# The order of the weight sums on VectorE in a feed-forward product by Strassen-like block sums

## The chip, the cores and the metric

The kernel runs on one core of one Trainium2 chip. Its matrix engine is TensorE (PE in the profile, with its weight loads as PEld); VectorE (DVE) and ScalarE (ACT) do the elementwise work, GpSimd (POOL) hardly any, and SyncE (SP) issues the DMAs. Each engine works through its own queue in order, and waits for the others by semaphores. The metric is the device time of one execution in microseconds.

## The reference

One layer of an encoder on 512 tokens of width 2048: a modulated norm, a mixer of two head groups, an output projection with a gated residual, and then the part this case is about, a SwiGLU feed-forward with D_FF = 5632:

```python
h = rms_norm(x, norm2_g[layer]) * (1.0 + sc2) + sh2
gate, up = jnp.split(h @ w_ffn_in[layer], 2, axis=-1)
x = x + g2 * ((jax.nn.silu(gate) * up) @ w_ffn_out[layer])
```

`h @ w_ffn_in` is the first feed-forward product, the multiplication by `w_ffn_out` the second. All is float32.

## The kernel before

**Float32 from three passes.** TensorE runs on a rounded float32 format. Every weight block is split into a high part, which is a cast on ScalarE (line 231), and a remainder, the block minus its high part, a subtraction on VectorE (line 232). The activations are split the same way beforehand. `product` (line 917) then multiplies high by high, high by remainder and remainder by high: for one product of 8 slices 24 matmuls of 128x128 by 128x256, all issued at line 93.

**Seven products in place of eight.** The columns of the hidden layer are worked off in 44 tiles of 128 gate columns and 128 up columns. The weights of a tile are four blocks of half the input width, A11 and A12 (gate, tile `wg`) and A21 and A22 (up, tile `wu`), and the tokens are in two halves of 256. Strassen's scheme in Winograd's form makes the 2x2 block product from seven half-size products and some sums. The sums of the activations are made once, before the loop. The sums of the weights are made for each tile on VectorE, in place: S1 = A21 + A22 (line 1138, in a buffer `ffS` of its own, one of three), A21 = A11 - A21 (1139), A11 = S1 - A11 (1140), A12 = A12 - A11 (1141).

**The loop over tiles** runs f from 2 to 43 (tiles 0 and 1 are done beforehand). In tile f the products come in the order 1, 2, 6, 7, 5, 4, 3, so that number 4 is the sixth in order. Product 1 uses A11 as loaded, 2 uses A12 as loaded, 6 the new A11, 7 the new A21, 5 S1, 4 A22, 3 the new A12. They go into three accumulators: A takes 1, 6, 5, 3; B takes 2; C takes 7 and 4. Where the scheme needs what an accumulator holds at some point, ScalarE copies it out (`tap`, line 1030): a after product 1, b after 6, c after 7, u after 5. The next product into the same accumulator may not start before the copy is done, so product 5 waits for the copy of b, product 4 for that of c.

**The tail of a tile** joins the taps: sg = B + a on VectorE (1163) and SiLU of it on ScalarE (1164), up = u + c (1165) and C + b (1166), SiLU of A (1167). `keep` (line 1078) multiplies the two (1084 for even tiles, 1086 for odd ones), makes four sums of each pair of tiles (1092 to 1096), splits them (1105 on ScalarE, 1106 on VectorE) and stores them through SP to memory (1108) as the operands of the second product. These jobs are spread over the next tiles by `one_later`. As B and a are complete early in the loop body's own tile, line 1163 of tile f runs in tile f itself; the final parts run in the next.

**Modulation rows.** While rows are left (tiles 2 to 17), the loop body ends with one row of the modulation, a load of 1 MB and a multiply with a sum of 2048 columns on VectorE (line 179, `ada`).

**Buffers for raw loads.** `wg`, `wu` and `ada` loads (1 MB each) share four buffers in turn. A buffer is free when its last reader is done: that of `wu` after the remainder of product 4, that of `wg` after the remainder of product 3, that of `ada` after line 179.

**What sets the order.** The kernel is traced as a program, and a scheduler orders each engine's queue: among the instructions whose inputs it takes to be ready it issues the one with the highest priority. Priority is the place in the program, and `high_priority(offset=n)` moves a block n places ahead. A tile is about 200 instructions, so with AHEAD = 300 the weight sums and the splits of a tile may be issued more than a tile early; taps stand at twice that. Line 1163 has no such offset. The scheduler works from its own estimates of when loads land. Once issued, a queue keeps that order on the chip. `issue_after(ins)` adds an edge of order alone: what the block traces on the engine of `ins` is queued behind `ins`.

```python
A21, A22 = halves_of(load(a["w_fi"][f, 1], [P, KT, P], f"wu{f}"))
S1 = tp.tile([P, HALF, P], F32, tag="sum", name=f"ffS{f}", bufs=3)
...
with tc.high_priority(offset=AHEAD):
    V.tensor_add(S1, A21, A22)
    V.tensor_sub(A21, A11, A21)
    V.tensor_sub(A11, S1, A11)
    V.tensor_sub(A12, A12, A11)
```

`split` (line 224) leaves in `last_lo` the subtraction that made the latest remainder.

Of the kernel before, what the change touches and what calls it, by code (L numbers as in the profile page):

```python
# [129 lines left out]
def trunk(ctx, tc, a):  # L130
    nc = tc.nc
    V, S, G = nc.vector, nc.scalar, nc.gpsimd
# [11 lines left out]
    def acc(name):  # L144
        return psum.tile([P, T], F32, tag="acc", name=name)

    def att(name):
        return psum.tile([P, T], F32, tag="att", name=name, bufs=2)
# [55 lines left out]
    def load(src, shape, name):  # L204
        r = raw_tile(shape, name + "r")
        nc.sync.dma_start(r, src)
        return r

    spare, count, home, last_lo = [], [0], [0], [None]
# [14 lines left out]
    def split(r, shape, name):  # L224
        count[0] += 1
        if spare and count[0] % 4 == 0:
            hi, lo = spare[0](shape, name)
        else:
            hi, lo = ring_pair(shape, name)
        with tc.high_priority(offset=AHEAD):  # L230
            S.copy(hi, r)  # L231
            last_lo[0] = V.tensor_sub(lo, r, hi.bitcast(F32)).ins  # L232
        return hi, lo
# [683 lines left out]
    def product(out, w, p, first=False):  # L917
        whi, wlo = w
        for j in range(HALF):
            PE.matmul(out, whi[:, j], H[p][:, j, 0], start=first and j == 0, stop=False, skip_group_check=True)  # L920
            PE.matmul(out, whi[:, j], H[p][:, j, 1], start=False, stop=False, skip_group_check=True)
            PE.matmul(out, wlo[:, j], H[p][:, j, 0], start=False, stop=j == HALF - 1, skip_group_check=True)
# [95 lines left out]
    def halves_of(r):  # L1018
        return r[:, 0:HALF], r[:, HALF:KT]

    def operand(raw, name, aside=True):
        home[0] = 48 if aside else 0
        return split(raw, [P, HALF, P], name)
# [3 lines left out]
    def tap(src, name):  # L1027
        t = tp.tile([P, HT], F32, tag="tap", name=name, bufs=4)
        with tc.high_priority(offset=2 * AHEAD):
            last_tap[0] = S.copy(t, src).ins  # L1030
        return t
# [24 lines left out]
    def begin_second():  # L1056
        places.append(fh.tile([P, 4, 4, 2, HT], F32R, tag="b1", name="opsA"))
        load_op(0, 0)
        load_y(0, 2)
        load_op(0, 1)  # L1060
        load_y(0, 0)
        yraw.append(hp.tile([P, 3, 4, T], F32, tag="hhi", name="yraw0"))
        load_y(0, 1)
        load_y(0, 3)
        load_op(0, 2)
        load_op(0, 3)
        places.append(hp.tile([P, 4, 4, 2, HT], F32R, tag="hlo", name="opsB"))
        for q in range(4, 7):
            load_op(0, q)
        yraw.append(fg.tile([P, 2, 4, T], F32, tag="b22", name="yraw"))  # L1070
# [7 lines left out]
    def keep(f, sg, up):  # L1078
        sgv, upv = (t.rearrange("p (h t) -> p h t", h=2) for t in (sg, up))
        if f % 2 == 0:  # L1080
            forms[0] = rp.tile([P, 8, HT], F32, tag="forms", name=f"forms{f}", bufs=1)
        R = forms[0]
        if f % 2 == 0:
            V.tensor_mul(R[:, 0:8:7], sgv, upv)
            return
        V.tensor_mul(R[:, 1:4:2], sgv, upv)
        n = f // 2
        c = max(c for c in range(len(CHUNKS)) if starts[c] <= n)

        def sums(a):  # L1090
            if a == 0:
                V.tensor_add(R[:, 4], R[:, 7], R[:, 3])
                V.tensor_sub(R[:, 5], R[:, 4], R[:, 0])
            else:
                V.tensor_sub(R[:, 6], R[:, 0], R[:, 7])
                V.tensor_sub(R[:, 2], R[:, 1], R[:, 5])

        def parts(a, b):
            q = slice(a, b)
            if f < FM - 1:  # L1100
                hi = tp.tile([P, b - a, HT], F32R, tag=f"fhi{a % 5}", name=f"fhi{f}_{a}", bufs=1)
            else:
                hi = cond[:, a * HT:b * HT].rearrange("p (q t) -> p q t", q=b - a).bitcast(F32R)
            with tc.issue_after(last_tap[0]):
                S.copy(hi, R[:, q])
            V.tensor_sub(R[:, q].bitcast(F32R), R[:, q], hi.bitcast(F32))  # L1106
            for i, t in enumerate((hi.bitcast(F32), R[:, q])):
                nc.sync.dma_start(opd[c][:, q, n - starts[c], i * HT:i * HT + HT], t)

        later.extend([partial(sums, 0), partial(sums, 1), partial(parts, 0, 3), None, partial(parts, 3, 5), None, partial(parts, 5, 7)])  # L1110
# [3 lines left out]
    def one_later():  # L1114
        job = later.pop(0) if later else None
        if job is not None:
            job()
# [10 lines left out]
    for f in range(2):  # L1128
        keep(f, held[:, 2 * f], held[:, 2 * f + 1])

    for f in range(2, FM):
        A11, A12 = halves_of(load(a["w_fi"][f, 0], [P, KT, P], f"wg{f}"))
        A21, A22 = halves_of(load(a["w_fi"][f, 1], [P, KT, P], f"wu{f}"))
        S1 = tp.tile([P, HALF, P], F32, tag="sum", name=f"ffS{f}", bufs=3)
        A, B, C = acc(f"ffA{f}")[:, 0:HT], acc(f"ffB{f}")[:, 0:HT], att(f"ffC{f}")[:, 0:HT]
        w1, w2 = operand(A11, f"ff{f}_1"), operand(A12, f"ff{f}_2")
        with tc.high_priority(offset=AHEAD):
            V.tensor_add(S1, A21, A22)
            V.tensor_sub(A21, A11, A21)
            V.tensor_sub(A11, S1, A11)  # L1140
            V.tensor_sub(A12, A12, A11)
        product(A, w1, 1, True)
        ta = tap(A, f"a{f}")
        one_later()
        product(B, w2, 2, True)
        one_later()
        product(A, operand(A11, f"ff{f}_6"), 6)
        tb = tap(A, f"b{f}")
        one_later()
        product(C, operand(A21, f"ff{f}_7"), 7, True)  # L1150
        t_c = tap(C, f"c{f}")
        one_later()
        product(A, operand(S1, f"ff{f}_5"), 5)
        tu = tap(A, f"u{f}")
        one_later()
        product(C, operand(A22, f"ff{f}_4"), 4)
        one_later()
        product(A, operand(A12, f"ff{f}_3", False), 3)

        sg = tp.tile([P, T], F32, tag="sg", name=f"sg{f}", bufs=2)  # L1160
        up = tp.tile([P, T], F32, tag="up", name=f"up{f}", bufs=1)
        with tc.high_priority(offset=2 * AHEAD if f == FM - 1 else 0):
            V.tensor_add(sg[:, 0:HT], B, ta)
            S.activation(sg[:, 0:HT], sg[:, 0:HT], AF.Silu)
            V.tensor_add(up[:, HT:T], tu, t_c)
            V.tensor_add(up[:, 0:HT], C, tb)
            S.activation(sg[:, HT:T], A, AF.Silu)
        if f == FM - 1:
            begin_second()
        with tc.high_priority(offset=2 * AHEAD if f == FM - 1 else 0):  # L1170
            keep(f, sg, up)
        if rest:
            rest.pop(0)()
# [20 lines left out]
    C = [wide[:, 0:T], wide[:, T:2 * T]]  # L1194
# [183 lines left out]
```

## Time and profile before

| | us |
|---|---|
| median of 3 runs | 2268.96 (2266.91 to 2269.43) |
| the profiled execution | 2268.31 |
| its span, first to last instruction | 2266.5 |
| tiles 7 to 43 of the first feed-forward product | 1103.70 to 1827.44 in the span |

The profile is one execution, recorded by instruction. Engines are busy or idle; where an engine sat idle before an instruction, the row says in brackets for how long and what released it. In rows of the timeline the first number is the start from the span's start and the second the duration. Neighbouring instructions of one engine overlap a little, so the step from start to start is shorter than the duration. `ff_5lo` and `ff_5hi` are the remainder and the cast of product 5; where the program's names have been shortened, `ff<-wu7r,ff` on line 232 is a remainder made from tile 7's `wu` (its first is product 7's, its second product 4's), and `ff<-wg7r,ff` one from `wg` (products 1, 2, 6 and 3 in this order). On PE the products are told by accumulator and operand: `ffA<-opA` is 1, `ffB<-opA` 2, `ffA<-opB` 6, `ffC<-opB` 7, `ffA<-opC` 5, `ffC<-opC` 4, `ffA<-opD` 3.

### The profile page before, as it was taken

Reading aid. Unit: us, or ns where it says so; the run is one execution under the profiler, and the core shown is the slowest. Engines: PE = TensorE matmul, PEld = TensorE weight load, DVE = VectorE, ACT = ScalarE, POOL = GpSimd, SP = SyncE. Lnnn points to the kernel's source line nnn. Section 1 sums busy time; section 2 is a strip of 40 time slices with the busy share of each in tenths; the row PEclk is TensorE's granted clock in tenths of the full one; section 3 lists DMA queues with packets and bytes.
Section 4 is the critical chain, followed back from the end, with each engine's and each line's share of the span. In section 5 each row is a group of like instructions: output and inputs, shape, how many; then the busy total and the mean of one; then the engine's idle time right before and its main releaser. Section 6 shows DMA issues by size and latency. Waiting matters only on the chain. (4 is left out here: it accounts for less than half of the span.)

```text
span 2266.5 us, 35532 instructions
## 1 busy us (share of the span) xinstructions
PE 2221.9 (98%) x14171; PEld 2025.4 (89%) x14171; DVE 1912.1 (84%) x2566; ACT 1157.3 (51%) x2015; POOL 10.1 (0%) x25
## 2 busy tenths in 40 slices
PE   7999899999999999999999999999999999999999
PEld 6899899978888888899999999999999987788887
DVE  8886778899888875599899988888888888898888
ACT  4315666566565622475444545555455554545453
POOL 0000000000000000000000000000000000000000
PEclk9999999999999999999999999999999999999999
DMA  9885546763232296326565554535454486666452
GB/s 371 314 319 215 178 142 232 288 228 112 93 112 75 83 327 250 111 103 228 205 215 201 195 181 145 176 131 177 142 172 150 159 333 248 241 223 223 163 198 67
DMA packets 115265, 437.68 MB, mean 193 GB/s; under 512 B 9854, under 2 KB 58268, under 8 KB 77340
## 3 DMA queue, kind: packets, MB, share of 16 engines
q1 hardware_dynamic: 115100, 435.42, 53.7%
q8 instruction: 111, 1.82, 0.3%
q14 instruction: 54, 0.44, 0.1%
HBM read 386.61 MB, written 48.77 MB: 192 GB/s over the span
## 5 line engine op out<-in xcount | busy, mean ns | idle before, releaser
L93 PE MATMUL sbp<-wsb,hhi 128*128 128x384 f32 x1024 | 271.2, 344 | 3.1 <-DVE wsb L232 1.7
L179 DVE SCALAR_TENSOR_TENSOR ada<-ada,cond 128x2048 f32<-128x2048 f32 x95 | 216.7, 2286 | 36.3 <-DMA ada<-in_w_ada 36.1
L93 PEld LDWEIGHTS sbp<-wsb,hhi 128*128 128x128 f32 x1024 | 186.3, 191 | 8.0 <-issue 3.3
L93 PE MATMUL sbp<-wsb,hlo 128*128 128x384 f32 x512 | 173.6, 339 | 0.0
L93 PE MATMUL wo<-ohi,wo 128*128 128x512 f32 x480 | 149.5, 391 | 2.0 <-ACT ohi L808 2.0
L232 DVE TENSOR_TENSOR wfo<-wfo,wfo 128x1024 fp32r<-128x1024 f32 (+1 forms) x72 | 83.5, 1163 | 31.7 <-ACT wfo L231 31.5
L93 PEld LDWEIGHTS wo<-ohi,wo 128*128 128x128 f32 x480 | 89.8, 188 | 21.0 <-ACT ohi L808 2.6
L231 ACT CAST wfo<-wfo 128x1024 fp32r<-128x1024 f32 (+1 forms) x72 | 72.5, 1007 | 63.2 <-PE foA L93 53.8
L93 PEld LDWEIGHTS sbp<-wsb,hlo 128*128 128x128 f32 x512 | 97.6, 191 | 0.8 <-issue 0.5
L93 PE MATMUL ffA<-opD,ff 128*128 128x256 f32 x768 | 97.3, 283 | 0.0
L93 PE MATMUL ffA<-opB,ff 128*128 128x256 f32 x768 | 93.3, 277 | 1.6 <-ACT ff L231 1.2
L93 PEld LDWEIGHTS ffA<-opD,ff 128*128 128x128 f32 x768 | 94.2, 191 | 0.0
L93 PE MATMUL ffC<-opC,ff 128*128 128x256 f32 x768 | 93.7, 278 | 0.4 <-ACT c L1030 0.4
L93 PE MATMUL wo<-olo,wo 128*128 128x512 f32 x240 | 93.3, 390 | 0.0
L93 PE MATMUL ffA<-opC,ff 128*128 128x256 f32 x744 | 90.3, 277 | 2.3 <-ACT b L1030 2.3
L93 PE MATMUL ffB<-opA,ff 128*128 128x256 f32 x768 | 92.4, 276 | 0.0
L93 PEld LDWEIGHTS ffA<-opB,ff 128*128 128x128 f32 x768 | 90.2, 189 | 2.0 <-ACT ff L231 1.4
L93 PEld LDWEIGHTS ffC<-opC,ff 128*128 128x128 f32 x768 | 90.3, 188 | 1.1 <-ACT c L1030 1.0
L93 PE MATMUL ffA<-opA,ff 128*128 128x256 f32 x744 | 89.7, 276 | 0.8 <-DVE ff L232 0.8
L93 PEld LDWEIGHTS ffA<-opC,ff 128*128 128x128 f32 x744 | 87.0, 188 | 3.2 <-ACT b L1030 3.1
L93 PEld LDWEIGHTS ffB<-opA,ff 128*128 128x128 f32 x768 | 89.5, 188 | 0.0
L93 PE MATMUL ffC<-opB,ff 128*128 128x256 f32 x744 | 89.5, 276 | 0.0
(1004 smaller groups left out, 5906.2 us busy)
## 6 DMA issues: line engine op xcount, KB each, us to landing
ada<-in_w_ada SPq DMA_DIRECT2D x95, 1024.0 KB, 6.0
wfo<-in_w_fo SPq DMA_DIRECT2D x16, 1024.0 KB, 5.0
yraw<-in_w_fo SPq DMA_DIRECT2D x16, 1024.0 KB, 5.0
fix<-in_w_fix SPq DMA_DIRECT2D x14, 1024.0 KB, 6.1
opd<-forms SPq DMA_DIRECT2D x44, 256.0 KB, 3.5
opd<-fhi SPq DMA_DIRECT2D x42, 256.0 KB, 4.2
opsC<-opd SPq DMA_DIRECT2D x10, 1024.0 KB, 6.6
opsA<-opd SPq DMA_DIRECT2D x9, 1024.0 KB, 5.7
```

The lines of the kernel that those rows point to most:

```text
L93: self.engine.matmul(out, lhsT, rhs, **kw)
L179: V.scalar_tensor_tensor(w, w, 1.0, row, op0=ALU.mult, op1=ALU.mult, accum_out=col)
L231: S.copy(hi, r)
L232: last_lo[0] = V.tensor_sub(lo, r, hi.bitcast(F32)).ins
```

## The change

From tile 3 on, S1 of tile f is queued on VectorE behind the remainder of product 4 of tile f - 1. The three other weight sums are not named by the edge; they read or write what S1 reads or writes. Loads, casts, products and the tail are as before.

```diff
+    fourth = None
     for f in range(2, FM):
...
         with tc.high_priority(offset=AHEAD):
-            V.tensor_add(S1, A21, A22)
+            if fourth is None:
+                V.tensor_add(S1, A21, A22)
+            else:
+                with tc.issue_after(fourth):
+                    V.tensor_add(S1, A21, A22)
             V.tensor_sub(A21, A11, A21)
             V.tensor_sub(A11, S1, A11)
             V.tensor_sub(A12, A12, A11)
...
-        product(C, operand(A22, f"ff{f}_4"), 4)
+        w4 = operand(A22, f"ff{f}_4")
+        fourth = last_lo[0]
+        product(C, w4, 4)
```

## The prediction

> **What bounds the kernel.** I start with the page's busy shares, then cut the first feed-forward product into stretches with the windows view (columns: length, then busy time of PE, PEld, DVE, ACT and POOL each with its count, the granted clock, DMA share, GB/s).
>
> ```profile
> PE 2221.9 (98%) x14171; PEld 2025.4 (89%) x14171; DVE 1912.1 (84%) x2566; ACT 1157.3 (51%) x2015; POOL 10.1 (0%) x25
> ...
> 1103.70:1346.07 242.37, 236.35 (x2018) 234.32 (x2017) 219.34 (x251) 116.73 (x175) 0.00 (x0) 0.99 0.57 200
> 1346.07:1614.87 268.80, 268.80 (x2354) 268.80 (x2353) 228.65 (x259) 139.89 (x203) 0.00 (x0) 1.00 0.46 158
> 1614.87:1635.44 20.57, 19.67 (x171) 19.47 (x169) 14.96 (x18) 9.44 (x14) 0.00 (x0) 1.00 0.51 182
> 1635.44:1827.44 192.00, 192.00 (x1683) 192.00 (x1682) 160.84 (x184) 99.30 (x145) 0.00 (x0) 1.00 0.49 168
> ```
>
> The cuts are starts of a tile's product 1 in the timeline. The second stretch holds tiles 19 to 32: 268.80 / 14 = 19.20 us a tile, and TensorE and its weight load are busy through all of it. The fourth holds tiles 34 to 43: 192.00 / 10 = 19.20 again. So 19.20 is the floor of a tile, set by TensorE, and no change on VectorE can go below it. The first stretch holds tiles 7 to 18: 242.37 against 12 x 19.20 = 230.40, so 11.97 us are lost there. The third is tile 33 alone: 20.57 - 19.20 = 1.37 lost. These 13.34 us are all that the loop has to give from tile 7 on. VectorE is busy 219.34 / 12 = 18.3 us a tile in the first stretch (each of those tiles up to 17 carries a modulation row, L179), but 228.65 / 14 = 16.3 in the second. What TensorE waited for, in the first stretch (three rows) and in tile 33 (the fourth):
>
> ```profile
> PE ffA L93 <- ACT b L1030: 5.2, 5, 2.6
> PE ffC L93 <- ACT c L1030: 0.4, 2, 0.2
> PE ffA L93 <- ACT a L1030: 0.4, 1, 0.4
> ...
> PE ffA L93 <- ACT b L1030: 0.9, 1, 0.9
> ```
>
> Nearly all is one wait: product 5 may not write its accumulator before ScalarE has copied product 6's result out ("b"). The longest is in tile 7; here is its timeline, DVE first, then ACT, then PE.
>
> ```profile
> 1110.27 0.42 DVE L1166 TENSOR_TENSOR up<-ffC,b 128x256 f32<-128x256 f32 x1
> 1112.98 1.23 DVE L1138 TENSOR_TENSOR ffS<-wu8r 128x1024 f32<-128x1024 f32 x1 [2.29 <-DMA wu8r<-in_w_fi]
> 1114.12 1.22 DVE L232 TENSOR_TENSOR ff_5lo<-ffS,ff_5hi 128x1024 fp32r<-128x1024 f32 x1
> 1115.26 1.22 DVE L1139 TENSOR_TENSOR wu8r<-wg8r,wu8r 128x1024 f32<-128x1024 f32 x1
> 1116.39 0.68 DVE L1106 TENSOR_TENSOR forms<-forms,fhi 128x512 fp32r<-128x512 f32 x1
> 1116.99 0.42 DVE L1163 TENSOR_TENSOR sg<-ffB,a 128x256 f32<-128x256 f32 x1
> 1117.33 1.21 DVE L232 TENSOR_TENSOR ff<-wu7r,ff 128x1024 fp32r<-128x1024 f32 x1
> ...
> 1117.44 0.42 ACT L1164 ACTIVATE sg<-sg 128x256 f32<-128x256 f32 x1 [6.37 <-DVE sg L1163]
> 1117.77 0.35 ACT L1030 COPY b<-ffA 128x256 f32<-128x256 f32 x1
> ...
> 1112.59 2.98 PE L93 MATMUL ffC<-opB,ff 128*128 128x256 f32 x24
> 1118.17 0.79 PE L93 MATMUL ffA<-opC,ff_5hi 128*128 128x256 f32 x2 [2.60 <-ACT b L1030]
> ```
>
> Read it upwards. Product 5 waits 2.60 for the copy of b; that copy stands in ScalarE's queue behind the SiLU, which waits 6.37 for the sum at L1163; and that sum stands on VectorE behind tile 8's weight sum (L1138), which held the queue 2.29 us for its load, and tile 8's difference (L1139). Both belong to the next tile. The row at 1117.33 is the remainder of product 4, sixth in order, behind which the change puts L1138. A second case, tile 14, has no load wait at all (PE, then DVE, then ACT):
>
> ```profile
> 1245.48 2.88 PE L93 MATMUL ffA<-opA,ff 128*128 128x256 f32 x24
> ...
> 1250.92 2.88 PE L93 MATMUL ffA<-opB,ff 128*128 128x256 f32 x24
> ...
> 1257.04 3.10 PE L93 MATMUL ffA<-opC,ff 128*128 128x256 f32 x24 [0.52 <-ACT b L1030]
> ...
> 1266.16 0.39 PE L93 MATMUL ffA<-opA,ff_1hi 128*128 128x256 f32 x2
> ...
> 1248.92 1.21 DVE L232 TENSOR_TENSOR ff<-wg14r,ff 128x1024 fp32r<-128x1024 f32 x1
> ...
> 1251.52 1.22 DVE L1138 TENSOR_TENSOR ffS<-wu15r 128x1024 f32<-128x1024 f32 x1
> ...
> 1253.26 1.22 DVE L1139 TENSOR_TENSOR wu15r<-wg15r,wu15r 128x1024 f32<-128x1024 f32 x1
> 1254.39 1.21 DVE L232 TENSOR_TENSOR ff<-ffS,ff 128x1024 fp32r<-128x1024 f32 x1
> 1255.53 0.42 DVE L1092 TENSOR_TENSOR forms<-forms 128x256 f32<-128x256 f32 x1
> 1255.87 0.41 DVE L1163 TENSOR_TENSOR sg<-ffB,a 128x256 f32<-128x256 f32 x1
> 1256.20 1.21 DVE L232 TENSOR_TENSOR ff<-wu14r,ff 128x1024 fp32r<-128x1024 f32 x1
> ...
> 1256.64 0.35 ACT L1030 COPY b<-ffA 128x256 f32<-128x256 f32 x1
> ```
>
> The tile ran from 1245.48 to 1266.16, 20.68 us, so 1.48 over the floor, of which the wait is only 0.52: after a wait the next products run slower too. Two products take 1250.92 - 1245.48 = 5.44, so 2.72 each.
>
> **The change, part by part.** No instruction is added or removed; an order edge is. Tile f+1's sum (L1138) must stand behind the remainder of product 4 of tile f, and three instructions come along because they use what it reads or writes: L1139 overwrites one of its inputs, L1140 reads its result, L1141 reads L1140's. The weight loads on SP are not in the edge.
>
> ```profile
> 1094.78 1.22 DVE L232 TENSOR_TENSOR ff<-wu6r,ff 128x1024 fp32r<-128x1024 f32 x1
> 1095.91 1.22 DVE L1138 TENSOR_TENSOR ffS<-wu7r 128x1024 f32<-128x1024 f32 x1
> ```
>
> For tile 7 the sum is already behind product 4 of tile 6, so the edge first binds for tile 8, and what TensorE loses before tile 7 stays.
>
> *What leaves the front.* In tile 7 the sum L1163 loses from ahead of it the wait 2.29, L1138 (1.14 from start to start) and L1139 (1.13): 4.56 us, from 1116.99 to 1112.43. The copy of b started 1117.77 - 1116.99 = 0.78 after the sum, so now at 1113.21, and ends 0.35 later; product 5 could start at 1112.59 + 2.72 = 1115.31: 1.75 us of room. In tile 14 the two take 2.27 away: the copy, 1256.64, becomes 1254.37, and product 5's own start, 1257.04 - 0.52 = 1256.52, is safe by 1.8 after 0.35 of copying. The casts these remainders need are there by then (ACT rows of tile 7, products 5 and 4):
>
> ```profile
> 1108.30 1.04 ACT L231 CAST ff_5hi<-ffS 128x1024 fp32r<-128x1024 f32 x1
> ...
> 1110.02 1.05 ACT L231 CAST ff<-wu7r 128x1024 fp32r<-128x1024 f32 x1
> ```
>
> What is late next is product 4's remainder: it cannot start before its cast ends at 1111.07, and it is needed only after product 5.
>
> *What arrives behind.* L1138 and L1139, 2.27 us, now stand between product 4's remainder and the rest of the tile: product 3's remainder, tile f+1's remainders 1 and 2, the modulation row, L1140, L1141 and remainder 6, which wait for them. The cover is twofold: product 4's remainder moves up by as much, and VectorE has a hole there.
>
> ```profile
> 1257.44 0.33 SPq L175 DMA_DIRECT2D ada<-in_w_ada  x1
> ...
> 1262.46 2.29 DVE L179 SCALAR_TENSOR_TENSOR ada<-ada,cond 128x2048 f32<-128x2048 f32 x1 [1.11 <-DMA ada<-in_w_ada]
> ```
>
> This load takes the buffer that product 4's remainder frees (1256.20 + 1.21 = 1257.41; issued 1257.44) and VectorE waits 1.11 for it. An earlier remainder issues it earlier on SP, and the two sums stand in the hole. I cost them at 0. If the cover is gone, remainder 6 feels it: in tile 14 it ends at 1248.92 + 1.21 = 1250.13, 0.79 before product 6 at 1250.92, so 2.27 - 0.79 = 1.48 a tile in the ten tiles 8 to 17, 14.8 us. A gain here is not counted, since nothing beats the floor. I take 0, because both casts above are done before the freed slot; 14.8 stays as the other end. Tiles 19 to 43 have 19.20 - 16.3 = 2.9 us idle on VectorE a tile: 0 as well.
>
> *The load wait.* By the time the sum now issues, near 1113, wu8 has landed (it ended the wait at 1112.98), so this wait goes and is not moved.
>
> *Half clock.* Behind the 2.60 wait TensorE ran slowly:
>
> ```profile
> 1117.90:1121.30 3.40, 3.13 (x14) 3.13 (x15) 2.65 (x4) 2.39 (x4) 0.00 (x0) 0.50 0.73 222
> ```
>
> 3.40 us at a granted 0.50 lose 1.7, already inside the 11.97. [...]
>
> *Sum.* Lost in tiles 7 to 18: 11.97. Not reached: tile 7's start to product 7, 1112.59 - 1103.70 = 8.89 against 3 x 2.72 = 8.16, so 0.73, which lies before any moved instruction. Left 11.24, and tile 33's 1.37: **12.61 us**. The profiled execution took 2268.31 (span 2266.5), so 2255.7; the median of the three runs, 2268.96, is 0.65 above it, so **2256.4**.
>
> **The rivals.** *Only the load wait goes*: L1163 is still queued behind L1138 and L1139, which are merely later. For it: its place is chosen by readiness, and it has no priority. Against: in tiles 7 and 14 it stands ahead of product 4's remainder. Then tile 14 keeps 1.48, and tile 7 keeps 2.60 - 2.29 = 0.31 and as much again of slow restart: about 2.1 less, with as much again unseen in other tiles perhaps; I say 10 gained, 2259.
>
> *The half clock was chance*: as a mechanism, its 1.7 is in the profiled execution and not in the median. Then 10.9 are gained from the median: 2258.1.
>
> *The cover is gone*: 14.8 come back, 2256.4 + 14.8 = 2271.2, no change that can be told.
>
> *Another head takes the queue.* With the two sums held back, VectorE is handed other ready work sooner, above all L1084, which waits for the stores of the previous forms. Its waits from 1346.07 to 1827.44:
>
> ```profile
> DVE forms L1084 <- DMA opd<-forms: 10.9, 11, 2.4
> ```
>
> Today it stands behind product 4's remainder (in tile 7 as well), where 2.4 us hurt nobody. Ahead of L1163 it would hold the SiLU and the copy of b as the load does in tile 33, at 1.37 a tile. It runs in every odd tile; from 9 to 43 that is 18, 24.7 us: 2256.4 + 24.7 = 2281.1. It decides from ten such tiles on (12.61 / 1.37 = 9.2). Against: its buffer is free only after the stores, which move with the rest.
>
> *Nothing moves*: excluded from tile 8 on, since both cases above show the sum ahead of product 4's remainder.
>
> **How the numbers follow.** Forecast 0.52; only the load wait 0.18; half clock 0.05; cover gone 0.13; other head 0.12. A measurement of this kernel tells about 0.2%, 4.5 us, from no change. Faster: 0.52 + 0.18 + 0.05 = 0.75; within: 0.13; slower: 0.12. The first three lie between 2256.4 and 2259, with the runs' own spread of 2.5 us (2266.91 to 2269.43) around it, and 0.73 below if tile 7's start goes too: from 2253.5. Above it reaches to 2265.5, some 60% of the way to the missing cover's 2271.2, which takes in half of that case, so that about 0.2 is left out.
>
> **What would show it.** Right: on VectorE L1138 directly behind product 4's remainder from tile 8 on, with no load wait; L1163 in tile 7 near 1112.4; no wait of product 5 for b; tiles 7 to 18 at about 231.1 us in all and tile 33 at 19.20; no half clock near 1118; the modulation row's wait shorter. Wrong: remainder 6 ending later than 5.44 us into a tile; L1084 waiting ahead of L1163; or the end of the loop earlier by 12 us with the total unchanged, a second product that does not follow.

## The result and the profile after

| | before | after |
|---|---|---|
| median of four runs each, us | 2267.99 (2266.91 to 2269.43) | 2255.11 (2253.16 to 2256.28) |
| ratio, 95% interval | | 0.9943 (0.9929 to 0.9957) |
| profiled execution / its span, us | 2268.31 / 2266.5 | 2256.16 / 2254.4 |

The changed kernel is 0.57% faster (0.43% to 0.71%). The forecast was 2256.4. The 2268.96 of the kernel before was the median of three runs; with a fourth it is 2267.99. Every engine has as many instructions as before, as the counts behind the x on the page's first line show:

```profile
PE 2216.3 (98%) x14171; PEld 2021.7 (90%) x14171; DVE 1916.6 (85%) x2566; ACT 1158.2 (51%) x2015; POOL 10.0 (0%) x25
```

The windows view of the changed kernel, cut at the same places as before (tiles 7 to 18, 19 to 32, 33, 34 to 43; columns as there: length, busy time of PE, PEld, DVE, ACT, POOL, granted clock, DMA share, GB/s):

```profile
1104.02:1335.63 231.61, 231.09 (x2019) 230.89 (x2017) 222.26 (x252) 119.52 (x175) 0.00 (x0) 1.00 0.60 213
1335.63:1604.43 268.80, 268.80 (x2355) 268.80 (x2353) 230.27 (x261) 138.97 (x203) 0.00 (x0) 1.00 0.45 159
1604.43:1623.63 19.20, 19.20 (x171) 19.20 (x169) 15.98 (x19) 9.56 (x14) 0.00 (x0) 1.00 0.39 139
1623.63:1815.63 192.00, 192.00 (x1683) 192.00 (x1682) 159.81 (x181) 98.81 (x145) 0.00 (x0) 1.00 0.49 168
```

Tiles 7 to 18 lose 231.61 - 230.40 = 1.21 us where they lost 11.97, and tile 33 is on its floor of 19.20. The loop ends at 1815.63 in place of 1827.44, 11.81 earlier, and the span is 12.1 shorter: what the loop gained was kept to the end. TensorE's waits from 1104.02 to the end of the loop are down to one row, and it is not one for b:

```profile
PE ffA L93 <- ACT a L1030: 0.5, 1, 0.5
```

The timeline of tile 7, DVE first, then ACT, PE and SP. The lines have moved: 1138 is 1143, 1139 is 1144, the sum 1163 is 1170, the SiLU 1171.

```profile
1111.09 1.22 DVE L232 TENSOR_TENSOR ff_5lo<-ffS,ff_5hi 128x1024 fp32r<-128x1024 f32 x1
1112.22 0.69 DVE L1106 TENSOR_TENSOR forms<-forms,fhi 128x512 fp32r<-128x512 f32 x1
1112.82 0.42 DVE L1170 TENSOR_TENSOR sg<-ffB,a 128x256 f32<-128x256 f32 x1
1113.16 1.22 DVE L232 TENSOR_TENSOR ff<-wu7r,ff 128x1024 fp32r<-128x1024 f32 x1
1114.29 1.22 DVE L1143 TENSOR_TENSOR ffS<-wu8r 128x1024 f32<-128x1024 f32 x1
1115.42 0.69 DVE L1084 TENSOR_TENSOR forms<-sg,up 128x512 f32<-128x512 f32 x1
1116.03 1.22 DVE L1144 TENSOR_TENSOR wu8r<-wg8r,wu8r 128x1024 f32<-128x1024 f32 x1
...
1119.77 2.28 DVE L179 SCALAR_TENSOR_TENSOR ada<-ada,cond 128x2048 f32<-128x2048 f32 x1
...
1113.28 0.42 ACT L1171 ACTIVATE sg<-sg 128x256 f32<-128x256 f32 x1 [1.72 <-DVE sg L1170]
1113.60 0.36 ACT L1030 COPY b<-ffA 128x256 f32<-128x256 f32 x1
...
1113.08 2.99 PE L93 MATMUL ffC<-opB,ff 128*128 128x256 f32 x24
...
1114.40 0.34 SPq L175 DMA_DIRECT2D ada<-in_w_ada  x1
```

The weight sum stands directly behind product 4's remainder and waits for nothing. The gate's sum and the copy of b come about 4.2 us earlier than before, the copy while product 7 still runs. The last row turns out to be worth as much: the load of the modulation row takes the buffer that product 4's remainder frees, and is issued at 1114.40, as soon as that remainder is done. Before, the same load was issued 4.17 us later:

```profile
1118.57 0.35 SPq L175 DMA_DIRECT2D ada<-in_w_ada  x1
```

VectorE's waits for loads in tiles 7 to 18, before (the longest five rows of seven):

```profile
DVE ada L179 <- DMA ada<-in_w_ada: 9.9, 10, 1.7
DVE ffS L1138 <- DMA wu19r<-in_w_fi: 2.4, 1, 2.4
DVE ffS L1138 <- DMA wu8r<-in_w_fi: 2.3, 1, 2.3
...
DVE ffS L1138 <- DMA wu18r<-in_w_fi: 1.6, 1, 1.6
DVE ffS L1138 <- DMA wu12r<-in_w_fi: 1.1, 1, 1.1
```

and after, all its waits for loads and stores:

```profile
DVE ada L179 <- DMA ada<-in_w_ada: 0.7, 1, 0.7
DVE forms L1084 <- DMA opd<-forms: 0.2, 1, 0.2
```

Two waits went, not one: the weight sum's (8.6 us over all its rows, now none) and the modulation row's (9.9, now 0.7).

### The profile page after: what moved, and what is told of

The parts are those of the page before. It is cut to its first block, busy times and chain, and to the rows that moved or that the text cites. A ratio compares the mean times of both kernels' runs of the same rounds, so it can differ in the third digit from the quotient of the medians.

```text
span 2254.4 us, 35505 instructions
## 1 busy us (share of the span) xinstructions
PE 2216.3 (98%) x14171; PEld 2021.7 (90%) x14171; DVE 1916.6 (85%) x2566; ACT 1158.2 (51%) x2015; POOL 10.0 (0%) x25
## 4 chain that ended last, share of the span: by engine, by line
PE 87%; DVE 8%; issue 2%; ACT 1%; DMA 1%; SPq 0%; DVEq 0%; ACTq 0%
PE ffA L93 21%; PE foA L93 10%; PE ffC L93 10%; PE sbp L93 7%; PE wo L93 7%; PE foC L93 5%; PE ffB L93 5%; PE st L93 4%; PE hgg L93 4%; PE hgf L93 3%; PE hgq L93 3%; PE foB L93 2%; DVE ada L179 1%; PE l L93 1%; PE sbo L93 1%
## 5 line engine op out<-in xcount | busy, mean ns | idle before, releaser
L232 DVE TENSOR_TENSOR wfo<-wfo,wfo 128x1024 fp32r<-128x1024 f32 (+1 forms) x72 | 83.5, 1164 | 31.7 <-ACT wfo L231 31.5
L231 ACT CAST wfo<-wfo 128x1024 fp32r<-128x1024 f32 (+1 forms) x72 | 72.5, 1007 | 63.2 <-PE foA L93 53.8
L93 PE MATMUL hgf<-hhi,whf 128*128 128x512 f32 x256 | 88.1, 402 | 0.0
```

What stands on the lines that cost most here:

```text
L93: self.engine.matmul(out, lhsT, rhs, **kw)
```

## The experiments

Two readings stood against each other. **Place**: the weight sum and the difference behind it stand ahead of the gate's sum, so the copy of b is late; whatever takes them out of the way, or takes the copy out from behind the SiLU, brings the gain. **Full queue**: in tiles with a modulation row VectorE's work and its waits for loads together come to more than the 19.20 us that TensorE needs, so VectorE falls behind, and the wait for b is only where that comes out; what shortens VectorE's waits or work brings the gain, and a new order that does not brings none. The table gives every kernel but the last of this section: its ratio to the kernel before with the 95% interval, and for tiles 7 to 18 VectorE's busy time, its waits for loads and stores (weight sum / modulation row / forms' stores), the sum of busy and waits, and what the tiles lost over 12 x 19.20 = 230.40.

| kernel | median | ratio | busy | waits | sum | lost |
|---|---|---|---|---|---|---|
| before | 2267.99 | | 219.3 | 8.6 / 9.9 / 0 | 237.8 | 11.97 |
| after | 2255.11 | 0.9943 (0.9929 to 0.9957) | 222.3 | 0 / 0.7 / 0.2 | 223.2 | 1.21 |
| after, again | 2256.12 | 0.9943 (0.9931 to 0.9956) | 222.5 | 0 / 0.4 / 0.3 | 223.2 | 1.88 |
| gate's sum by priority | 2272.28 | 1.0021 (1.0010 to 1.0031) | 220.5 | 5.6 / 3.6 / 9.8 | 239.5 | 14.00 |
| SiLU behind the copy | 2267.17 | 0.9999 (0.9989 to 1.0008) | 218.3 | 9.1 / 12.4 / 0 | 239.8 | 14.01 |
| the edge in tile 8 alone | 2265.13 | 0.9991 (0.9981 to 1.0000) | 219.4 | 7.0 / 10.3 / 0 | 236.7 | 10.19 |
| edge behind product 5 | 2259.21 | 0.9951 (0.9938 to 0.9965) | 221.0 | 0.6 / 12.6 / 0 | 234.2 | 5.17 |
| row behind remainder 6 | 2260.28 | 0.9963 (0.9949 to 0.9977) | 220.2 | 10.8 / 0 / 3.3 | 234.3 | 4.86 |
| rows from tile 20 | 2268.64 | 1.0005 (0.9991 to 1.0020) | 197.2 | 3.7 / 0 / 3.0 | 203.9 | 0 |
| weight sum twice | 2261.99 | 0.9974 (0.9963 to 0.9985) | 230.9 | 3.3 / 0 / 1.7 | 235.9 | 6.87 |
| edge behind product 3 | 2253.47 | 0.9939 (0.9924 to 0.9954) | 218.2 | 6.1 / 0 / 2.6 | 226.9 | 0 |
| the same, again | 2256.05 | 0.9942 (0.9929 to 0.9954) | 218.3 | 3.9 / 0 / 2.6 | 224.8 | 0.62 |

Read the last two columns together: where the sum is under 230.40, the tiles lose at most 1.9 us; where it is over, they lose 4.9 or more, and by and large more the further it is over. Two kinds of waits are not in the sum. VectorE's waits for ScalarE's casts are longest where it has least to do (1.8 us before, 6.5 after, 24.8 with the rows from tile 20). Some waits of line 1084 are put on no load or store (2.3 us before; 3.8, 2.6 and 1.5 in the kernels "gate's sum by priority", "SiLU behind the copy" and "the edge in tile 8 alone"); they would only raise sums that are over 230.40 as it is. A wait is partly an outcome of the tiles' pace, so the table alone is no proof of cause; the experiments that change one term are.

### The gate's sum forward by priority, no edge

```diff
+        with tc.high_priority(offset=2 * AHEAD):
             V.tensor_add(sg[:, 0:HT], B, ta)
```

> The kernel before with one change: the sum sg = B + a (L1163) gets a priority offset of 600, so it may be queued as soon as its inputs are ready. The weight sums keep their place, so S1 still waits for its load on VectorE. Theory (what cost time was the chain sum, SiLU, copy of b, product 5): the waits of product 5 go and the time falls by 8 to 12 us to about 2256 to 2260. Rival (the load wait itself costs VectorE time that TensorE feels): the load waits stay, and so does the time, 2265 to 2269.

The ratio is 1.0021: slightly slower. In ten of the tiles 7 to 18 priority did not move the sum past the others; one of them is tile 9, here in this kernel's timeline of VectorE (the gate's sum is L1164):

```profile
1151.04 1.23 DVE L1138 TENSOR_TENSOR ffS<-wu10r 128x1024 f32<-128x1024 f32 x1 [1.68 <-DMA wu10r<-in_w_fi]
1152.19 0.42 DVE L1167 TENSOR_TENSOR up<-ffC,b 128x256 f32<-128x256 f32 x1
1152.52 1.22 DVE L1139 TENSOR_TENSOR wu10r<-wg10r,wu10r 128x1024 f32<-128x1024 f32 x1
1153.65 1.22 DVE L232 TENSOR_TENSOR ff<-ffS,ff 128x1024 fp32r<-128x1024 f32 x1
1154.79 0.42 DVE L1164 TENSOR_TENSOR sg<-ffB,a 128x256 f32<-128x256 f32 x1
```

It still stands behind both weight sums. Only in tiles 10 and 14 does it stand ahead of them; these two are on the floor, but as the tiles in front of them lost 2.48 and 1.56 us, they decide nothing. That the scheduler did not count it as ready when it placed them is the likely reason; only the order is shown. What did move is the product of the even tiles, which now stands where it waits for stores:

```profile
DVE forms L1084 <- DMA opd<-forms: 9.8, 3, 3.4
```

So the experiment hardly made what it was meant to make, and says little on Place. It does show the prediction's rival "another head takes the queue" at work: 9.8 us in three waits, with the sum of busy and waits at 239.5 and the loss at 14.00.

### The SiLU behind the copy of b

```diff
         tb = tap(A, f"b{f}")
+        b_copy = last_tap[0]
...
-            S.activation(sg[:, 0:HT], sg[:, 0:HT], AF.Silu)
+            with tc.issue_after(b_copy):
+                S.activation(sg[:, 0:HT], sg[:, 0:HT], AF.Silu)
```

> The kernel before with one order edge on ScalarE and none on VectorE: the SiLU of L1164 is queued behind the copy of b. S1 keeps its place and its load waits, and the sum L1163 stays as late as it is. Theory (ScalarE's queue is the link through which a late sum reaches TensorE): product 5 no longer waits for b, 9 to 12 us less, 2256 to 2259; what product 4 lost to the copy of c in tile 17 (0.6) may stay. Rival (VectorE's lost time is what TensorE feels, by late remainders): no gain, 2265 to 2269.

TensorE's waits in tiles 7 to 18 of this kernel, all of them:

```profile
PE ffC L93 <- ACT c L1030: 4.7, 4, 1.8
PE ffA L93 <- ACT a L1030: 2.8, 3, 1.4
```

No wait for b is left, and the time is the same: 0.9999. The waits for c and for a have taken its place, 7.5 us for the 5.2 that b had, and the tiles lose 14.01. In tile 10 product 4 waits 1.67 us for the copy of c. On ScalarE that copy, at 1179.22, stands behind the SiLU and, ahead of it, a cast of the forms that waits 3.54 us for another sum of VectorE:

```profile
1177.23 0.83 ACT L1105 CAST fhi<-forms 128x768 fp32r<-128x768 f32 x1 [3.54 <-DVE forms L1096]
```

So the chain that the prediction read backwards from product 5 (copy, SiLU, gate's sum, weight sums) is real, but it is an outlet: with it closed, the delay of VectorE comes out at the next copy.

### The edge in tile 8 alone

The changed kernel with the edge for tile 8 only:

```diff
-            if fourth is None:
+            if f != 8:
                 V.tensor_add(S1, A21, A22)
```

> The change for one tile only: S1 of tile 8 behind the remainder of product 4 of tile 7. Theory (each tile's loss is its own): tile 7 loses its stall, 4.6 us by the prediction's working, the other tiles keep theirs, so about 2263 to 2264. Rival (the gain is slack that builds up from tile to tile): clearly less than 4 us, or, if one good tile is enough to put all that follow back on the floor, the full 12.

The windows view, tile 7 and then tiles 8 to 18:

```profile
1104.72:1125.22 20.50, 19.89 (x170) 19.69 (x169) 20.50 (x25) 9.22 (x14) 0.00 (x0) 1.00 0.79 272
1125.22:1345.31 220.09, 216.67 (x1850) 214.28 (x1849) 198.92 (x227) 107.24 (x161) 0.00 (x0) 1.00 0.56 195
```

Tile 7 took 24.49 before (1103.70 to 1128.19), so the one edge gains 3.99 there. Tiles 8 to 18 lose 220.09 - 211.20 = 8.89, where before they lost 11.97 - 5.29 = 6.68 (5.29 is what tile 7's 24.49 is over the floor). So 2.21 of the 3.99 are lost again in the tiles behind: the gain is not handed on, and the loss is not each tile's own. The time, 0.9991 (0.9981 to 1.0000), cannot tell so small a gain from none.

### One wait without the other: the edge behind product 5, and the row behind remainder 6

Behind product 5's remainder the weight sum is still ahead of product 4's remainder, so the row's buffer comes free no earlier:

```diff
-        product(A, operand(S1, f"ff{f}_5"), 5)
+        w5 = operand(S1, f"ff{f}_5")
+        fourth = last_lo[0]
+        product(A, w5, 5)
...
-        fourth = last_lo[0]
         product(C, w4, 4)
```

> The change with the edge one remainder earlier: S1 behind the remainder of product 5 (the fifth) of the tile in front, so the two sums stand ahead of product 4's remainder again and the modulation row's load is not freed sooner. Theory now (VectorE's busy time plus its waits for loads exceeds 19.20 us in the tiles with a row; the change took away both S1's wait and the row's): S1's load wait mostly goes, the row's wait of about 1 us a tile stays, tiles 7 to 18 lose 2 to 8 us in place of 11.97, 2257 to 2264. Rival (what counts is the place of the two sums ahead of the sum L1163): L1163 stands behind them in most tiles, and the loss stays above 9 us, 2264 to 2269.

The complement, in the kernel before without the edge: the modulation row is taken from the end of the loop body and queued behind remainder 6 of the next tile.

```diff
+        w6 = operand(A11, f"ff{f}_6")
+        if f > 2 and rest:
+            with tc.issue_after(last_lo[0]):
+                rest.pop(0)()
-        product(A, operand(A11, f"ff{f}_6"), 6)
+        product(A, w6, 6)
...
-        if rest:
-            rest.pop(0)()
```

> The kernel before, without the edge on S1; the modulation row of each tile is queued on VectorE behind the remainder of product 6 of the next tile (one order edge), when its load has long landed. It is the complement of the run with the edge behind product 5, where S1's waits went and the row's stayed. Theory (all load waits of VectorE in tiles 7 to 18 count alike, and about 7 us of them are free): the row's 9.9 falls below 3, S1's wait stays at 7 to 12, tiles 7 to 18 lose 2 to 6 us in place of 11.97, total 2257 to 2263. Rival (S1's waits alone made the loss, since they stand ahead of the sum L1163): the loss stays above 9 us, 2265 or more. Rival (the row's waits alone made it): on the floor, 2255 to 2257.

Edge behind product 5, VectorE's waits for loads in tiles 7 to 18 and the window of these tiles:

```profile
DVE ada L179 <- DMA ada<-in_w_ada: 12.6, 8, 2.2
...
DVE ffS L1143 <- DMA wu8r<-in_w_fi: 0.4, 1, 0.4
DVE ffS L1143 <- DMA wu16r<-in_w_fi: 0.2, 1, 0.2
...
1102.35:1337.92 235.57, 233.84 (x2018) 232.86 (x2017) 221.02 (x252) 116.70 (x175) 0.00 (x0) 1.00 0.59 209
```

Row behind remainder 6, the same window:

```profile
1103.77:1339.03 235.26, 234.61 (x2019) 233.61 (x2017) 220.22 (x248) 117.79 (x174) 0.00 (x0) 1.00 0.60 207
```

In the first the weight sum stands ahead of the gate's sum in all twelve tiles, as before, and the difference (line 1144) in six of them. The weight sum's waits are gone all the same (0.6 left of 8.6), and the row's have stayed (12.6); in the second the row's are gone and the weight sum's have stayed (10.8). Each loses about 5 of the 11.97: 5.17 and 4.86. By its loss over the floor, either wait's going brings 6.8 to 7.1 us, and the change, which takes both, brings 10.8. Beside the kernel before on the same chip the ratios, 0.9951 and 0.9963, lie between those of before and after; their intervals overlap that of the change in part, so that the split rests on the windows.

### The rows moved to other tiles: rows from tile 20

```diff
-        if rest:
+        if rest and f > 19:
             rest.pop(0)()
```

in the kernel before. This is the experiment that decides between Place and Full queue: the edge is not there, the weight sums are where they were, and VectorE has ten rows less to do in tiles 7 to 18.

> The kernel before, without the edge, with the sixteen modulation rows in tiles 20 to 35 in place of 2 to 17. Theory (over-full VectorE): tiles 7 to 18 run on the floor of 19.20 or within 1.5 us of it in all, though S1 and its load wait stand where they stood, and tiles 20 to 36 lose 6 to 14 us; the total is within 6 us of before. Rival (place of the two sums): tiles 7 to 18 keep most of their 11.97, and the rows add more in tiles 20 to 36: 2270 or above.

Its windows, tiles 7 to 18 and then the 16 tiles 20 to 35:

```profile
1105.22:1335.62 230.40, 230.40 (x2019) 230.40 (x2017) 197.22 (x223) 119.62 (x174) 0.00 (x0) 1.00 0.45 158
1354.82:1677.80 322.98, 313.86 (x2690) 310.80 (x2689) 289.54 (x327) 153.82 (x233) 0.00 (x0) 1.00 0.57 200
```

Tiles 7 to 18 lose nothing. In tile 7 of this kernel, VectorE:

```profile
1105.47 1.23 DVE L1138 TENSOR_TENSOR ffS<-wu8r 128x1024 f32<-128x1024 f32 x1 [0.19 <-DMA wu8r<-in_w_fi]
...
1108.08 1.22 DVE L1139 TENSOR_TENSOR wu8r<-wg8r,wu8r 128x1024 f32<-128x1024 f32 x1
...
1110.95 0.42 DVE L1163 TENSOR_TENSOR sg<-ffB,a 128x256 f32<-128x256 f32 x1
```

Both weight sums stand ahead of the gate's sum, here and in each of the tiles 7 to 18, as in the kernel before. But VectorE is not behind, so the gate's sum comes 5.73 us into the tile in place of 13.29 (1116.99 - 1103.70). The loss went with the rows: tiles 20 to 35 lose 322.98 - 16 x 19.20 = 15.78, and before they lost none outside tile 33. The total is the same, 1.0005. Place alone costs nothing; place in a full queue does. With the rows their loads left these tiles too (158 GB/s in place of 200), and the weight sum's waits fell from 8.6 to 3.7, so this run does not part VectorE's work from its waits. The next adds work alone.

### Work added: the weight sum made twice

In the changed kernel, tiles 8 to 17 and 24 to 33, the weight sum is made a second time, with the same value:

```diff
                 with tc.issue_after(fourth):
                     V.tensor_add(S1, A21, A22)
+                    if 8 <= f < 18 or 24 <= f < 34:
+                        V.tensor_add(S1, A21, A22)
```

> The changed kernel with S1 added twice, the second time over itself, in tiles 8 to 17 and 24 to 33: 1.14 us more of VectorE in each, the value unchanged. Theory (VectorE is full in tiles with a row, 18.3 of 19.20, and has 2.9 us over in those without): tiles 7 to 18 lose 2 to 6 us more than the 1.21 of the changed kernel, tiles 24 to 34 nothing; 2257 to 2261. Rival (VectorE has room everywhere once S1 is out of the way): both stretches stay on the floor, 2254 to 2256.

The windows, tiles 7 to 18 and then the ten tiles 24 to 33:

```profile
1101.71:1338.98 237.27, 234.20 (x2019) 232.77 (x2018) 230.89 (x260) 117.76 (x175) 0.00 (x0) 1.00 0.61 208
1434.98:1626.97 191.99, 191.99 (x1682) 191.99 (x1681) 174.10 (x195) 99.23 (x145) 0.00 (x0) 1.00 0.45 158
```

Ten sums of 1.14 us, 11.4 in all (the window's busy time grows by 8.6, as its ends cut off other work), bring back 6.87 - 1.21 = 5.7 us of loss in the tiles with rows and nothing in those without. So the change did not make the order immune; it made room, and about half of what was added no longer fitted.

### The edge behind product 3's remainder

```diff
         w4 = operand(A22, f"ff{f}_4")
-        fourth = last_lo[0]
         product(C, w4, 4)
...
-        product(A, operand(A12, f"ff{f}_3", False), 3)
+        w3 = operand(A12, f"ff{f}_3", False)
+        fourth = last_lo[0]
+        product(A, w3, 3)
```

> The change with the edge one remainder later: S1 behind the remainder of product 3 (the seventh) of the tile in front. Theory (VectorE has room behind product 4's remainder): still on the floor of 19.20 us a tile, within 2 us of the changed kernel, 2254 to 2258. Rival (the cover is thin: in tiles 8 to 17 remainder 6 comes too late when the two sums move 2 us further back): tiles 8 to 17 lose 0.5 to 1.5 us each, 2260 to 2270.

The window of tiles 7 to 18:

```profile
1101.41:1331.81 230.40, 230.40 (x2019) 230.40 (x2017) 218.19 (x248) 118.80 (x175) 0.00 (x0) 1.00 0.60 212
```

Nothing is lost, although the weight sum waits 6.1 us for its loads: with the row's waits at none, 218.2 + 8.7 = 226.9 still fits under 230.40. A wait of VectorE is thus not a cost as such. Against the kernel before, the ratio is 0.9939 (0.9924 to 0.9954); whether it beats the change was tried by one more run of both on the same chip:

> The version with the edge behind product 3's remainder again. Theory (what it has over the changed kernel is the 1.2 to 1.5 us that tiles 6 and 7 lose there): 1 to 2 us below the changed kernel. Rival: the difference seen so far, 2253.47 against 2255.11, is the scatter of the first tile: equal within 0.5 us.

> The changed kernel again, beside the version with the edge behind product 3, on the same chip: 2253 to 2257, ratio to before 0.994 to 0.995.

The medians are 2256.05 and 2256.12. The profile of product 3's edge has fewer tiles off the floor, but the 1 us that this could be worth is not told apart in the time.

### The forms of the first two tiles later

On top of the edge behind product 3, the joins (`keep`) of tiles 0 and 1, made ahead of the loop, were moved into tile 2, the first of the loop, which takes 24.36 us:

```diff
-    for f in range(2):
-        keep(f, held[:, 2 * f], held[:, 2 * f + 1])
...
         tu = tap(A, f"u{f}")
+        if f == 2:
+            for g in range(2):
+                keep(g, held[:, 2 * g], held[:, 2 * g + 1])
```

> The version with the edge behind product 3's remainder, and the two keep calls of tiles 0 and 1 (multiplications of 0.6 us each on VectorE) moved from ahead of the loop into tile 2, behind product 5. Theory (tile 2 waits for VectorE's weight sums, ahead of which these two stand): tile 2, 24.4 us there, loses 0.6 to 1.2 us, 2252 to 2253. Rival (the held values keep a load buffer longer, so the next loads are late): tiles 3 and 4 lose 1 us or more, 2254 to 2257.

Tile 2 took 24.34, and the ratio is 0.9936 (0.9923 to 0.9950) beside 0.9939: a miss. These jobs are not what holds tile 2. In both kernels TensorE waits in this tile 1.4 and 1.2 us for casts of ScalarE (L231) and 0.8 for a remainder of VectorE (L232); no run took these waits away, so what holds the tile stays open.

## Why the prediction held, and where its reasons did not

**The sum** (11.97 - 0.73 + 1.37 = 12.61) measured 11.97 - 1.21 + 1.37 = 12.13 from tile 7 on. Tile 7 began 0.32 later, so the loop ends 11.81 earlier. The **floor** held: no tile went under 19.20, and 268.80 for tiles 19 to 32 is unchanged. What stayed is 1.21 where 0.73 was foretold; of it 1113.08 - 1104.02 - 8.16 = 0.90 falls ahead of product 7, where the 0.73 was, with the same wait for a (0.4 before, 0.5 now), and the other 0.31 behind it, where products go on at 2.83 us.

**What leaves the front** held almost to the row. The gate's sum of tile 7 was foretold at 1112.43 and came at 1112.82, the copy of b at 1113.21 and came at 1113.60: both 0.39 late, 0.32 of which is the tile's later start. **The load wait** went and was not moved. **Half clock**: none came in tile 7, where the stall went too: tiles 7 to 18 ran at a granted clock of 1.00. That the clock differs between executions of one kernel is borne out: over the span it was 0.994 to 0.997 in twelve executions of the kernel before on one chip, and behind stalls of the same length the slow stretch differed in two profiles of the changed kernel (last section). That the half clock of tile 7 comes in some executions and not in others is not shown. How much of the 1.7 us is in the medians is not known; it is within the interval of the ratio.

**"Nearly all is one wait" is the step that failed**, as a cause and not as a number. With the wait for b taken away alone, the time stayed at 0.9999 and product 4 waited for c and product 6 for a. The prediction's second case misled it: tile 14 "has no load wait at all", and its lateness was put down to the place of the two sums. But with the rows elsewhere the sums kept their place and the tiles lost nothing. VectorE had come into tile 14 late: the remainder of product 6 started 1248.92 - 1245.48 = 3.44 us into the tile, but 0.33 in the changed kernel and 0.62 ahead of the tile with the rows elsewhere. That this delay was carried over from waits for rows and loads in the tiles in front is the likely reading, not shown for this tile; the 2.21 us lost again behind tile 8's edge fit it.

**"What arrives behind" was priced at 0, and is part of the gain.** The earlier load of the modulation row was seen, but as cover for two sums of 2.27 us. It took away 9.2 us of VectorE's waits, more than the weight sum's 8.6, and alone it is worth about as much (4.86 lost where the row's wait alone went, 5.17 where the weight sum's alone went). The number held since the prediction summed what the tiles lose, whatever the cause, and the change removed both. That is in part luck: by its working the same sum would have stood for a change that takes away the wait for b alone, and that one gained nothing.

**The rivals.** "Only the load wait goes" comes nearest to the edge behind product 5: 6.8 of 11.97 gained in tiles 7 to 18, by its windows. "The cover is gone" did not happen: in tiles 8 to 17 of the changed kernel remainder 6 starts 1.38 us into the tile at the latest and takes 1.22, against the limit of 5.44. By its busy time alone VectorE has 230.40 - 219.34 = 11.1 us to spare in these tiles. "Another head" did not happen in the changed kernel (L1084 waits 0.2) but did in the kernel with priority, at 9.8. "The half clock was chance" would give 2258.1 where 2255.11 was measured; that the granted clock differs between executions is borne out (0.994 to 0.997), its price is not, and it is the least well excluded.

## What to carry to other kernels

Sum the busy time and the load waits of the second-busiest engine over the stage and hold them against the bound engine's floor. In this kernel, where they came to more, the wait that the bound engine showed was only the outlet, and closing it moved the loss to the next copy. Where two loads share a ring of buffers, put the work that awaits one of them behind the work that frees the buffer of the other: here one edge shortened two waits. Here a wait was free as long as the sum stayed under the floor.

## What the runs showed of the hardware

A stall of TensorE of 2.60 us was followed by 3.40 us at a granted clock of 0.50 in the kernel before; one of 2.01 us in the kernel with priority was not. Here are the half clock in tile 7 of the kernel before and the part of tile 9 of the kernel with priority that holds its stall:

```profile
1117.89:1121.30 3.41, 3.13 (x14) 3.13 (x15) 2.66 (x4) 2.40 (x4) 0.00 (x0) 0.50 0.73 221
...
1145.87:1165.55 19.68, 17.67 (x153) 17.47 (x152) 14.73 (x17) 9.52 (x15) 0.00 (x0) 1.00 0.55 198
```

In tile 2 TensorE stalls twice, by 1.61 and 1.23 us in the kernel before and by 1.42 and 1.23 in the changed kernel, and the granted clock falls to 0.50 there in both, for 3.41 us from 1012.07 in the first and for 6.82 from 1009.19 in the second. These are the two half clocks:

```profile
1012.07:1015.48 3.41, 3.41 (x18) 3.41 (x17) 3.41 (x4) 0.84 (x1) 0.00 (x0) 0.50 0.28 113
...
1009.19:1016.01 6.82, 6.21 (x29) 6.21 (x30) 6.82 (x11) 2.46 (x3) 0.00 (x0) 0.50 0.40 150
```

Two profiles of the changed kernel have these stalls alike and what follows not. The first, then the second (1.41 and 1.24):

```profile
1008.07 0.51 PE L93 MATMUL ffC<-opB,ff_7hi 128*128 128x256 f32 x2 [1.42 <-ACT ff_7hi L231]
1009.80 0.80 PE L93 MATMUL ffA<-opB,ff 128*128 128x256 f32 x2 [1.23 <-ACT ff L231]
...
1014.24 3.56 PE L93 MATMUL ffA<-opB,ff 128*128 128x256 f32 x22
...
1008.68 0.50 PE L93 MATMUL ffC<-opB,ff_7hi 128*128 128x256 f32 x2 [1.41 <-ACT ff_7hi L231]
1010.41 0.50 PE L93 MATMUL ffA<-opB,ff 128*128 128x256 f32 x2 [1.24 <-ACT ff L231]
...
1014.40 2.75 PE L93 MATMUL ffA<-opB,ff 128*128 128x256 f32 x22
```

The stalls agree to 0.01 us, but the same 22 matmuls of product 6 took 3.56 us in one and 2.75 in the other. What decides whether a stall is followed by a half clock, and for how long, is not shown.

At a granted clock of 1.00 a whole tile ran slower than the floor, 19.82 us, with no wait in it. Tiles 7 and 8 of the second run of product 3's edge:

```profile
1104.11:1123.93 19.82, 19.82 (x170) 19.82 (x169) 18.28 (x21) 8.87 (x14) 0.00 (x0) 1.00 0.69 248
1123.93:1143.13 19.20, 19.20 (x170) 19.20 (x169) 19.20 (x24) 11.23 (x16) 0.00 (x0) 1.00 0.56 191
```

TensorE is busy through both, but a product takes 19.82 / 7 = 2.83 us in the first and 19.20 / 7 = 2.74 in the second. The prediction had seen this only after a wait. The tile in front of the slow one, tile 6, already took 19.78, and its products were slow from the fourth on. The slower row has more DMA traffic, 248 GB/s against 191, but traffic alone does not make it: with the edge in tile 8 alone, a tile without a row ran as slowly at 160.

```profile
1480.00:1499.83 19.83, 19.83 (x170) 19.83 (x169) 18.21 (x21) 10.34 (x15) 0.00 (x0) 1.00 0.47 160
```

The cause stays open.
